# An idle tile at the right end of SBUF grows from 32 to 416 bytes a partition, in a one-core encoder layer

## The chip, the core and the metric

The kernel runs on one core of a Trainium2 chip. The metric is the device time of one execution in microseconds, as the median of several runs. On-chip memory (SBUF) has 128 partitions; an address below is a byte offset within a partition, the same in all of them. TensorE (PE in the profile) multiplies a 128x128 block of weights, loaded by an instruction of its own (PEld), with a stream of up to 512 columns, and writes to PSUM. DVE, ACT and POOL are the vector, scalar and GpSimd engines, and SP issues transfers.

## What is computed

One layer of an encoder on a 1024 x 1024 float32 activation: a feed-forward half step, a mixing step of two groups of attention heads, and a second feed-forward half step, each between two RMS norms.

```python
def swiglu(x, w_gate, w_up, w_down):
    return (jax.nn.silu(x @ w_gate) * (x @ w_up)) @ w_down      # d_ff = 2816

h = swiglu(rmsnorm(x, ffn1_pre_g), ffn1_w_gate, ffn1_w_up, ffn1_w_down)
x = x + 0.5 * rmsnorm(h, ffn1_post_g)
h = rmsnorm(x, mix_pre_g)
q, k, v = split(h @ w_qkv)                     # 16 heads of 64
o_na = neighbourhood_attention(q[:8], k[:8], v[:8], na_rel_bias)
o_dil = dilated_mixture_attention(q[8:], k[8:], v[8:], t5_rel_bias)
mixed = concat(rmsnorm(o_na, na_out_g), rmsnorm(o_dil, dil_out_g)) @ w_out
x = x + rmsnorm(mixed, mix_post_g)
h = swiglu(rmsnorm(x, ffn2_pre_g), ffn2_w_gate, ffn2_w_up, ffn2_w_down)
x = x + 0.5 * rmsnorm(h, ffn2_post_g)
```

## The kernel before

**Products.** Every float32 operand is split into a high part and a remainder (`hi`, `lo`), and one product of 128 x 128 weights and 512 columns becomes three on TensorE: hi x hi, hi x lo, lo x hi (`mm3`, lines 340 to 344; the profile's L342, L343 and L344). In the code's calls of `matmul(out, a, b)`, `a` is the weights (stationary) and `b` the stream (moving).

**Seven instead of eight.** The large matrix products are cut into 2 x 2 blocks and done in a scheme with seven block products of sums and differences, named A11, A12, S1, S2, S3, S4 and A22 after their left operand. The x operand of each is held in SBUF as a `hi` and a `lo` tile of 8192 bytes a partition (class `Operand`): A11 and A12 in the pool `xa`, the other five in `xb`.

**Gate and up products** (`PairGemm`, PSUM tiles `mmp`). One pass over 22 blocks in each FFN, and over 8 blocks for q and k. Weights are the streamed-in matrices, and the 512 columns of x are the stream. In `ahead` (lines 481 to 516) A11 and A12 of the first 10 blocks (8 for q and k) are done early, with weights split into the pool `wr`, or, in the second FFN and for q and k, into the pool `p0` for every third block (line 470 ff.). Then `run` (lines 561 to 625) does the remaining products block by block: an early block has S2, S1, S3, S4 and A22, a late one all seven. In late blocks the order on TensorE is A11, A22 of the block before, S2, A12, S1, S3, S4; each is 4 steps of k times three products, 12 products of 512 columns. Weights for S2, S1 and S3 (`T2`, `T1` in the code) are split into the pool `wt`; those for A11, A12, S4 and A22 into `wr`. While a block's products run, ACT and DVE split the next block's weights (L441, L442) out of the raw tiles of `wg`, and DVE forms their sums and differences (L530 to L532). The first two blocks of the first FFN do A11 in two halves of 256 columns.

**Down and value products** (`Passes`, PSUM tiles `accp`). Here the seven products run as seven passes, and both operands (`pw`) are fetched and split into tiles of the pool `pr` (L722, L723), except in the value passes, where x of `Operand` is the weights and `pw` alone is the stream. In the value passes the first fetch of A11 goes to `p0` (`pw0hi`, `pw0lo`) and the second to a tile of `xb`.

**Attention.** Per head: scores (`sp`, L1121 and L1239), softmax, transposes (`ptp`, L1038), copies to `pt` (L1040) in the pool `ptp`, and products with v (`po`, L1142 and L1255) of 128 columns. v is held in `va` and `vb`, or `vs`, from the pool `vp0`, for every second pair of dilated heads from `op`.

**Order.** The order on TensorE is the program's. The other engines' order is found by the framework, with some places tied by hand. A tile may take the place of earlier ones as soon as those are done with; this wait is found tile by tile, from the addresses (`reuse_waits="tile"`).

**Where tiles lie.** Pools are stacked from both ends of SBUF. From the left: 16,384 bytes that are reserved, 128 bytes of constants, the identity (512 bytes, at 16,512), and the pool `small` (960 bytes), so that the next left pool begins at 17,984, which is 35 x 512 + 64. From the right end, 229,344, first comes the tile `edge` with 32 bytes, so that the next right pool ends at 229,312, which is 447 x 512 + 448. Tiles of products and their raw inputs have sizes that are multiples of 512, hence all left ones lie at 64 modulo 512 and all right ones at 448, with the exceptions in the table.

| tiles | end | address modulo 512 |
|---|---|---|
| x of S1, S2, S3, S4, A22 (`xb`); `wr`, `pr`, `pw`; `sp`, `cp`; operands of the output projection | left | 64 |
| x of A11, A12 (`xa`); `wt` of the two FFNs; `p0`; `wg` and `tj` while the blocks run; `st` (pool `stk`), `vp0`, `og` | right | 448 |
| `wt` and `wg` for q and k after the early blocks | left | 64 |
| `pt` (pool `ptp`), `s` and `sb` (pool `pp`), two of four `pb` | right, behind `at` with 1,152 bytes | 320 |
| `q`, `va`, `vb` of the pool `op`, behind two `ob` of 4,224 bytes | left | 320 |
| identity (the stream of the transposes) | left | 128 |

The lines that the change touches are 1332, where `edge` is made, and 1746 and 1747, where the pools `at`, `pp` and `ptp` are opened, all in `layer`.

Of the kernel before, what the change touches and what calls it, by code (L numbers as in the profile page):

```python
# [10 lines left out]
F32 = mybir.dt.float32  # L11
# [8 lines left out]
P, T = 128, 512  # L20
# [1292 lines left out]
def layer(tc, a, out):  # L1313
    nc = tc.nc
    c = Ctx(tc)
    with ExitStack() as ctx:
        def pool(name, bufs, stack=ctx, **kw):
            return stack.enter_context(tc.tile_pool(name=name, bufs=bufs, reuse_waits="tile", **kw))
# [10 lines left out]

        c.dr = pool("dr", 1, space=bass.MemoryType.DRAM)  # L1330
        c.base = pool("base", 1)
        pool("edge", 1, side="right").tile([P, 8], F32, name="edge")
        c.small = pool("small", 4)
        c.ident = c.base.tile([P, P], F32, name="ident")
        make_identity(nc, c.ident)
# [409 lines left out]
        og = c.og = [ogp.tile([P, 8, 512], F32, name=f"og{g}") for g in range(2)]  # L1745
        for n, b in (("at", 2), ("pp", 4), ("ptp", 3)):
            setattr(c, n, pool(n, b, s4, side="right"))
        for n, b, st in (("pst", 2, s7), ("pss", 3, s5), ("pso", 2, s5), ("psm", 1, s5)):
            setattr(c, n, pool(n, b, st, space=PSUM))
        xo = {}  # L1750
# [198 lines left out]
```

## Time and profile before

| | |
|---|---|
| median of 3 runs | 1877.63 us (1876.08 to 1878.42) |
| the profiled execution | 1875.7 us |
| its span in the profile | 1873.9 us, 25125 instructions |
| mean granted TensorE clock | 0.998 of full speed |
| products of 128x512 as `mmp` | 3 lines x 1464 less 3 x 16 of 256 columns |
| products of 128x512 as `accp` | 3 lines x (600 + 104 + 128 + 24) |

Stages, as the trace has them: up to 445 us the gate and up products of the first FFN (the early A11 and A12 up to 60), then its down passes to some 640, v and q, k to 910, attention to 1130, output projection to 1220, gate and up of the second FFN to 1655, down passes to the end.

How to read it: a group of instructions is a line of the code, an engine, an operation, and output <- inputs by tile names with numbers left out; then count, busy time, mean duration in ns of one, and the idle time before them with what ended it. Products are pipelined, so a duration overlaps the next product's; the distance from start to start is what a product takes. The profile shows tile names, no addresses; those come from the pools, as above.

### The profile page before, as it was taken

Reading aid. Unit: us, or ns where it says so; the run is one execution under the profiler, and the core shown is the slowest. Engines: PE = TensorE matmul, PEld = TensorE weight load, DVE = VectorE, ACT = ScalarE, POOL = GpSimd, SP = SyncE. Lnnn points to the kernel's source line nnn. Section 1 sums busy time; section 2 is a strip of 40 time slices with the busy share of each in tenths; the row PEclk is TensorE's granted clock in tenths of the full one; section 3 lists DMA queues with packets and bytes.
Section 4 is the critical chain, followed back from the end, with each engine's and each line's share of the span. In section 5 each row is a group of like instructions: output and inputs, shape, how many; then the busy total and the mean of one; then the engine's idle time right before and its main releaser. Section 6 shows DMA issues by size and latency. Waiting matters only on the chain.

```text
span 1873.9 us, 25125 instructions
## 1 busy us (share of the span) xinstructions
PE 1837.1 (98%) x8904; PEld 1527.2 (81%) x8904; DVE 1332.9 (71%) x2247; ACT 829.3 (44%) x1485; POOL 321.1 (17%) x504
## 2 busy tenths in 40 slices
PE   8999999999999999999999999999999999999998
PEld 6787888887888887878899997877888888878886
DVE  6878777776466877577777856788886777754558
ACT  6522233334443656133688765563223333344333
POOL 2123111111121122132333100120111111110000
PEclk9999999999999999999999999999999999999999
DMA  7656455546889857769686522584554566486564
GB/s 281 235 167 218 147 211 203 219 180 236 312 294 312 288 206 245 256 209 304 201 276 223 186 96 101 192 303 153 187 179 166 181 213 230 179 325 203 193 227 141
DMA packets 171808, 406.52 MB, mean 217 GB/s; under 512 B 19921, under 2 KB 42353, under 8 KB 169634
## 3 DMA queue, kind: packets, MB, share of 16 engines
q1 hardware_dynamic: 123842, 244.23, 39.3%
q0 software_dynamic: 46832, 158.59, 23.0%
q10 hardware_dynamic: 1008, 2.10, 0.3%
q8 instruction: 70, 1.15, 0.2%
q14 instruction: 56, 0.46, 0.1%
HBM read 278.39 MB, written 131.52 MB: 219 GB/s over the span
## 4 chain that ended last, share of the span: by engine, by line
PE 73%; issue 12%; DVE 8%; DMA 3%; ACT 2%; POOL 1%; SPq 0%; DVEq 0%; POOLq 0%; ACTq 0%
PE mmp L344 16%; PE mmp L343 16%; PE mmp L342 16%; PE accp L343 5%; PE accp L344 5%; PE accp L342 5%; PE po L1142 2%; PE po L1255 2%; PE ptp L1038 2%; DMA x<-x 1%; PE sp L1239 1%; DVE pw L723 1%; PE sp L1121 1%; PE trp L173 1%; DVE x L290 1%
## 5 line engine op out<-in xcount | busy, mean ns | idle before, releaser
L342 PE MATMUL mmp<-x,whi 128*128 128x512 f32 (+1 forms) x1464 | 578.3, 395 | 4.4 <-ACT whi L441 3.0
L344 PE MATMUL mmp<-x,wlo 128*128 128x512 f32 (+1 forms) x1464 | 575.7, 393 | 3.6 <-DVE wlo L442 3.6
L343 PE MATMUL mmp<-x,whi 128*128 128x512 f32 (+1 forms) x1464 | 575.2, 393 | 0.8 <-DVE x L181 0.7
L342 PEld LDWEIGHTS mmp<-x,whi 128*128 128x128 f32 x1464 | 276.4, 189 | 68.4 <-issue 3.4
L344 PEld LDWEIGHTS mmp<-x,wlo 128*128 128x128 f32 x1464 | 276.4, 189 | 68.2 <-DVE wlo L442 5.9
L343 PEld LDWEIGHTS mmp<-x,whi 128*128 128x128 f32 x1464 | 276.5, 189 | 63.0 <-DVE x L181 1.6
L723 DVE TENSOR_TENSOR pw<-praw,pw 128x1024 fp32r<-128x1024 f32 (+1 forms) x181 | 200.5, 1149 | 120.1 <-ACT pw L722 119.8
L722 ACT CAST pw<-praw 128x1024 fp32r<-128x1024 f32 (+1 forms) x181 | 168.5, 981 | 209.3 <-PE accp L344 171.7
L343 PE MATMUL accp<-pw 128*128 128x512 f32 x600 | 233.7, 389 | 3.4 <-DVE pw L723 3.4
L441 ACT CAST whi<-wraw 128x1024 fp32r<-128x1024 f32 x128 | 134.4, 1051 | 230.0 <-PE mmp L343 223.4
L342 PE MATMUL accp<-pw 128*128 128x512 f32 x600 | 234.4, 391 | 0.5 <-DVE hb L779 0.5
L344 PE MATMUL accp<-pw 128*128 128x512 f32 x600 | 233.6, 389 | 0.0
L442 DVE TENSOR_TENSOR wlo<-wraw,whi 128x1024 fp32r<-128x1024 f32 x128 | 157.2, 1230 | 22.3 <-ACT whi L441 22.1
L343 PEld LDWEIGHTS accp<-pw 128*128 128x128 f32 x600 | 112.7, 188 | 27.2 <-DVE pw L723 4.2
L342 PEld LDWEIGHTS accp<-pw 128*128 128x128 f32 x600 | 112.6, 188 | 24.4 <-issue 0.9
L344 PEld LDWEIGHTS accp<-pw 128*128 128x128 f32 x600 | 112.6, 188 | 23.4
L619 DVE TENSOR_TENSOR c<-mmp,u 128x512 f32<-128x512 f32 x52 | 36.0, 692 | 90.0 <-PE mmp L344 90.0
L667 POOL DMA_DIRECT2D g<-sg x44 | 23.9, 543 | 443.7 <-DVE sg L660 263.2
L441 ACT CAST whi<-traw 128x512 fp32r<-128x512 f32 x52 | 32.3, 621 | 151.2 <-DVE traw L531 106.8
L460 ACT COPY s<-mmp 128x512 f32<-128x512 f32 x52 | 30.6, 588 | 133.5 <-PE mmp L344 122.4
L530 DVE TENSOR_TENSOR wraw<-wraw 128x1024 f32<-128x1024 f32 x52 | 63.5, 1222 | 8.7 <-DMA wraw<-in_wu_dram 7.7
L605 DVE TENSOR_TENSOR c<-mmp,v 128x512 f32<-128x512 f32 x52 | 35.8, 689 | 35.9 <-PE mmp L344 34.8
(282 smaller groups left out, 2768.5 us busy)
## 6 DMA issues: line engine op xcount, KB each, us to landing
praw<-g SPq DMA_DIRECT2D x70, 512.0 KB, 5.9
wraw<-in_wg_dram SPq DMA_DIRECT2D x44, 512.0 KB, 4.3
wraw<-in_wu_dram SPq DMA_DIRECT2D x44, 512.0 KB, 6.6
tr<-in_wd_dram SPq DMA_DIRECT2D x44, 512.0 KB, 6.4
g<-sg POOLq DMA_DIRECT2D x88, 256.0 KB, 5.2
ts<-tr POOLq DMA_DIRECT2D x22, 1024.0 KB, 4.7
praw<-ts SPq DMA_DIRECT2D x88, 256.0 KB, 4.0
praw<-in_wd_dram SPq DMA_DIRECT2D x66, 256.0 KB, 5.9
```

Source lines behind the costliest of these rows:

```text
L342: nc.tensor.matmul(out, ahi, bhi, start=start, stop=False, skip_group_check=go_on)
L343: nc.tensor.matmul(out, ahi, blo, start=False, stop=False, skip_group_check=go_on)
L344: nc.tensor.matmul(out, alo, bhi, start=False, stop=stop, skip_group_check=go_on)
L441: nc.scalar.copy(hi, raw)
L442: nc.vector.tensor_sub(lo, raw, hi.bitcast(F32))
L530: nc.vector.tensor_sub(r[:, 0:2], r[:, 1:3], r[:, 0:2])
L619: nc.vector.tensor_add(c21, d, u2)
L722: nc.scalar.copy(hi, raw[:, :m])
L723: nc.vector.tensor_sub(lo, raw[:, :m], hi.bitcast(F32))
L1038: nc.tensor.transpose(ps[:, j, :], src[:, j * P:(j + 1) * P], c.ident)
L1142: nc.tensor.matmul(po[:, un * 2 + j], pt[:, 2 * j + t, :], rhs, start=t == 0, stop=t == 1)
L1255: nc.tensor.matmul(po[0][:, u], pt[0][:, j, :], vs[:, k0 + j, :], start=j == 0, stop=j == n - 1)
```

## The change

```diff
@@ -1329,7 +1329,7 @@
 
         c.dr = pool("dr", 1, space=bass.MemoryType.DRAM)
         c.base = pool("base", 1)
-        pool("edge", 1, side="right").tile([P, 8], F32, name="edge")
+        pool("edge", 1, side="right").tile([P, 104], F32, name="edge")
         c.small = pool("small", 4)
         c.ident = c.base.tile([P, P], F32, name="ident")
         make_identity(nc, c.ident)
@@ -1745,6 +1745,8 @@
         og = c.og = [ogp.tile([P, 8, 512], F32, name=f"og{g}") for g in range(2)]
         for n, b in (("at", 2), ("pp", 4), ("ptp", 3)):
             setattr(c, n, pool(n, b, s4, side="right"))
+            if n == "at":
+                c.at.tile([P, 96], F32, tag="edge", name="edge", bufs=1)
         for n, b, st in (("pst", 2, s7), ("pss", 3, s5), ("pso", 2, s5), ("psm", 1, s5)):
             setattr(c, n, pool(n, b, st, space=PSUM))
         xo = {}
```

The tile `edge` takes 416 bytes instead of 32, so every tile from the right end lies 384 bytes lower, at 64 modulo 512 where it lay at 448. In the attention the pool `at` gets a tile of 384 bytes that nothing reads or writes; `pp` and `ptp`, stacked behind it, lie 768 bytes lower in all, at 64 where they lay at 320. Left tiles stay, those of `op` at 320 among them. The lowest tile of `ptp` then begins at 124,480, where the left tile `hs` of the output projection ends. No instruction is added or removed.

## The prediction

> **What bounds the kernel now.** I read the page's busy times first, then the chain of waits, then the costliest groups, and last the stretches and single products that these point to.
>
> ```profile
> span 1873.9 us, 25125 instructions
> PE 1837.1 (98%) x8904; PEld 1527.2 (81%) x8904; DVE 1332.9 (71%) x2247; ACT 829.3 (44%) x1485; POOL 321.1 (17%) x504
> PE 73%; issue 12%; DVE 8%; DMA 3%; ACT 2%; POOL 1%; SPq 0%; DVEq 0%; POOLq 0%; ACTq 0%
> ```
>
> PE has something in flight for 98% of the span and is 73% of the chain that ended last. Only 1873.9 - 1837.1 = 36.8 us of the span has no product in it. So a time can change in two ways: the products get closer together or farther apart, or a wait appears. The groups say which products these are:
>
> ```profile
> L342 PE MATMUL mmp<-x,whi 128*128 128x512 f32 (+1 forms) x1464 | 578.3, 395 | 4.4 <-ACT whi L441 3.0
> L344 PE MATMUL mmp<-x,wlo 128*128 128x512 f32 (+1 forms) x1464 | 575.7, 393 | 3.6 <-DVE wlo L442 3.6
> L343 PE MATMUL mmp<-x,whi 128*128 128x512 f32 (+1 forms) x1464 | 575.2, 393 | 0.8 <-DVE x L181 0.7
> L342 PEld LDWEIGHTS mmp<-x,whi 128*128 128x128 f32 x1464 | 276.4, 189 | 68.4 <-issue 3.4
> L343 PE MATMUL accp<-pw 128*128 128x512 f32 x600 | 233.7, 389 | 3.4 <-DVE pw L723 3.4
> L342 PE MATMUL accp<-pw 128*128 128x512 f32 x600 | 234.4, 391 | 0.5 <-DVE hb L779 0.5
> L344 PE MATMUL accp<-pw 128*128 128x512 f32 x600 | 233.6, 389 | 0.0
> ```
>
> The same 128x512 product has a mean of 393 to 395 ns as `mmp` and 389 to 391 ns as `accp`, and neither group waits for anyone worth naming (4.4 us at most in 1464). A duration here holds the product's tail under the next one, so the distance between starts is the real price; it is read from stretches and start times:
>
> ```profile
> 250.00:445.00 195.00, 195.00 (x844) 158.20 (x843) 142.62 (x171) 65.99 (x90) 26.51 (x45) 1.00 0.56 204
> 500.00:600.00 100.00, 100.00 (x443) 82.84 (x442) 61.54 (x64) 41.10 (x52) 19.01 (x24) 1.00 0.83 286
> 1700.00:1800.00 100.00, 100.00 (x443) 82.81 (x442) 49.57 (x52) 41.34 (x52) 0.00 (x0) 1.00 0.58 193
> ```
>
> The columns are the stretch, its length, then busy time and count of PE, PEld, DVE, ACT and POOL, the granted clock, and DMA. PE is never idle in the three, and the clock is full. A stretch also counts products cut at its ends, up to two: 195 us over 843 is 231.3 ns a product in the gate products, 100 us over 441 is 226.8 ns in the passes. The same product, at the same clock, is 4.5 ns dearer in one stage than in the other.
>
> **Which products are the dear ones.** In the late blocks of a gate GEMM the runs are known from the code (S1 and S3 with 24 products, then S4, A11, the last block's A22, S2, A12 with 12 each), so the first product of each run can be found in the order of time:
>
> ```profile
> 330.91 0.40 PE L342 MATMUL mmp<-x,whi 128*128 128x512 f32 x1
> ...
> 336.50 0.40 PE L342 MATMUL mmp<-x,whi 128*128 128x512 f32 x1
> ...
> 339.26 0.40 PE L342 MATMUL mmp<-x,whi 128*128 128x512 f32 x1
> ...
> 342.05 0.39 PE L342 MATMUL mmp<-x,whi 128*128 128x512 f32 x1
> ...
> 344.79 0.40 PE L342 MATMUL mmp<-x,whi 128*128 128x512 f32 x1
> ...
> 347.59 0.39 PE L342 MATMUL mmp<-x,whi 128*128 128x512 f32 x1
> ...
> 350.36 0.40 PE L342 MATMUL mmp<-x,whi 128*128 128x512 f32 x1
> ```
>
> Now lay the addresses beside it. Left tiles lie at 64 modulo 512, right ones at 448. S1 and S3 take weights from `wt` (right) and x from `xb` (left): 5.59 us for 24, or 232.9 ns. A11 (weights left, x right) takes 2.79 us for 12, 232.5 ns; S2 (weights right, x left) 2.80, 233.3 ns; A12 2.77, 230.8 ns. I call these 60 **mixed**; together 13.95 us, 232.5 ns each. S4 and A22 have both operands on the left: 2.76 us, 230.0 ns, and 2.74 us, 228.3 ns. They come right behind mixed runs; the passes, where nothing is mixed, have 226.8. So the price goes with the two residues differing, and a run of equal residues needs a dozen products or more to come down.
>
> Is it the residue, or which end of SBUF an operand lies in? In the value passes the first fetched pair has both at 448: weights are x of A11 (right), the stream is `pw0` out of `p0` (right).
>
> ```profile
> 674.62 0.39 PE L342 MATMUL accp<-pw0hi,x 128*128 128x512 f32 x1
> ...
> 679.83 0.39 PE L344 MATMUL accp<-pw0hi,x 128*128 128x512 f32 x1
> ```
>
> From the first to the 24th start are 5.21 us, 226.5 ns a product: 448 with 448 is as quick as 64 with 64. These weights lie near 196,500 to 208,300 and the stream near 129,000 to 137,000. Later in the value passes both are on the left, far apart: x of S2, S1 and S4 as weights between 18,000 and 84,000, the stream out of `pr` between 138,800 and 159,300.
>
> ```profile
> 766.00 0.39 PE L342 MATMUL accp<-pw,x 128*128 128x512 f32 x1
> ...
> 786.40 0.39 PE L342 MATMUL accp<-pw,x 128*128 128x512 f32 x1
> ```
>
> 20.40 us for 90 products, 226.7 ns. So a long distance costs nothing, and wherever a border between two parts of SBUF might lie, from 18,000 to 208,300, one of these two pairs crosses it without a price. The residue is what is left.
>
> **The change part by part.** No instruction is added, removed or moved: two tiles that nobody reads or writes grow or appear. What moves is addresses. Every right tile goes down by 384 bytes, 448 to 64; `pp` and `ptp` go down by 768, 320 to 64. All 512-column products then have equal residues.
>
> Count of mixed products (12 for each run of four k, times three). Each FFN: S2, S1, S3 in 22 blocks, 792, and A11, A12 in the 12 late blocks, 288; twice that is 2160. A11 and A12 of the early blocks: first FFN 10 x 24 less the 24 that run as halves of 256 columns, 216; second FFN 6 x 24 = 144, since four blocks have their weights in `p0`, right as x is; q and k 5 x 24 = 120 (their `wt` is left). Value passes 72 of 336. Sum 2712 of the 6912 products of 512 columns.
>
> Term 1, mixed products: 232.5 - 226.7 = 5.8 ns each. I leave out the 192 of q, k and v, whose stretch is not bound by PE:
>
> ```profile
> 640.00:780.00 140.00, 137.35 (x623) 111.23 (x622) 99.26 (x164) 75.10 (x125) 35.78 (x60) 1.00 0.74 254
> 697.46 6.81 DMA graw<-in_wqk_dram
> 740.76 6.07 DMA qk<-qk
> ```
>
> The two lower rows are pieces of the chain of waits there, start and length: it runs through DMAs, 1.1 us at stake (192 x 5.8). So 2520 x 5.8 = 14.6 us.
>
> Term 2, runs of equal residues behind mixed ones: S4 and A22 lose (230.0 - 226.7) x 12 = 40 ns and (228.3 - 226.7) x 12 = 19 ns a block. Over 44 blocks, 2.6 us come back.
>
> Term 3, the other way: a run that starts after short products is out of step as well. Between the products stand transposes, in groups of four:
>
> ```profile
> L173 PE MATMUL trp<-ident,x 128*128 128x128 f32 x144 | 21.8, 276 | 2.5 <-DVE x L290 1.6 <-DVE x L221 0.5 <-ACT raw L255 0.4
> L173 PE MATMUL trp<-ident,xn 128*128 128x128 f32 x48 | 7.9, 298 | 1.7 <-DVE xn L1586 0.9 <-DVE x L290 0.8
> ```
>
> That is 192 / 4 = 48 groups. If each leaves the next run to settle at S4's 40 ns, 1.9 us stay. Bounds: 0 if it settles at once, 3.8 if it takes twice as long; I take the middle since S4 is the nearest row.
>
> Small products of the attention change residues too, and some pairs that agree now will differ (`pt` goes 320 to 64, while `va` and `vb` out of the pool `op` stay at 320). The two rows are `vb` out of `vp0` (448, differs from `pt`) and out of `op` (320, the same):
>
> ```profile
> L1142 PE MATMUL po<-vb,pt 128*128 128x128 f32 x64 | 8.5, 275 | 0.0
> ...
> L1142 PE MATMUL po<-vb,pt 128*128 128x128 f32 x32 | 4.2, 275 | 0.0
> ```
>
> 275 ns both ways: no price, a zero that needs no cover.
>
> DVE and ACT keep their operands' sizes. Their rows with one residue for all (L723 in the passes, mostly left) and with two (L442, `wraw` right and `whi` left or right):
>
> ```profile
> L723 DVE TENSOR_TENSOR pw<-praw,pw 128x1024 fp32r<-128x1024 f32 x153 | 182.9, 1233 | 116.7 <-ACT pw L722 116.4
> L442 DVE TENSOR_TENSOR wlo<-wraw,whi 128x1024 fp32r<-128x1024 f32 x128 | 157.2, 1230 | 22.3 <-ACT whi L441 22.1
> L722 ACT CAST pw<-praw 128x1024 fp32r<-128x1024 f32 x153 | 153.2, 1047 | 201.4 <-PE accp L344 170.1 <-DMA praw<-in_wd_dram 19.5 <-DMA praw<-g 6.1
> L441 ACT CAST whi<-wraw 128x1024 fp32r<-128x1024 f32 x128 | 134.4, 1051 | 230.0 <-PE mmp L343 223.4 <-issue 4.0 <-DMA sgt<-sgd 2.1
> ```
>
> 0.3% apart: nothing. Waits for a reused place: right tiles now begin where left tiles end (both 64 modulo 512) instead of 384 bytes above, so a right tile laps over as many old left tiles as before or one fewer. No wait can be added between them; I count zero.
>
> Sum: 14.6 + 2.6 - 1.9 = 15.3 us. A second way, from the groups' means: mmp (395 + 393 + 393) / 3 = 393.7 against accp 389.7, 4.0 ns over 4392 products, is 17.6 us, without term 3. The profiled execution took 1875.7 us, 1.8 us of it outside its span; 1875.7 - 15.3 = 1860.4. The median of the three runs is 1.9 us higher, so **1862.3 us**.
>
> [...]
>
> **Rivals.** A (partly): the products close up, but where PE already waits, others take the gain. PE's gaps are in three more stretches:
>
> ```profile
> 25.00:60.00 35.00, 34.10 (x158) 27.29 (x158) 26.73 (x55) 23.99 (x40) 9.36 (x18) 1.00 0.86 315
> 60.00:250.00 190.00, 186.38 (x799) 149.18 (x798) 147.74 (x198) 55.98 (x77) 45.02 (x81) 0.99 0.56 188
> 1200.00:1290.00 90.00, 86.37 (x400) 69.15 (x399) 70.97 (x119) 52.85 (x90) 21.57 (x40) 1.00 0.71 250
> ```
>
> DVE is at 76 to 79% there, which speaks for it; that PE's idle is 4% or less speaks against. Mixed there: 216 + 10 blocks x 36 + 144 = 720, 4.2 us lost, so 1866.5.
>
> B (not the residue): the 5.8 ns hang on something that the shift leaves, as on weights and stream coming from two pools. For it: in every mixed run the two come from different ends. Against: S1 of the value passes takes weights from `xb` and its stream from `pr`, two pools far apart, at 226.7. Nothing would change: 1877.6.
>
> C (slower): with all residues equal, the streams of PE meet those of DVE and ACT, which now lie at 64 too, in the gate stage's splits. Price: if all 6912 products then cost the mixed price, the 4200 cheap ones lose 5.8 ns, 24.4 us, so 1877.6 + 24.4 = 1902.0; it decides from 15.3 us / 6912 = 2.2 ns a product. Against: between 500 and 600 us raw, split and streamed operands all are left tiles, DVE is busy for 61.54 and ACT for 41.10 us, and the product takes 226.8.
>
> **How the numbers follow.** Forecast 0.78, A 0.12, B 0.06, C 0.04. Faster or slower begins at 0.2%, 3.8 us, about what a measurement of this kernel can tell from no change. Forecast and A are faster: 0.90; B is within: 0.06; C is slower: 0.04. The range: at the low end all of 17.6, the 1.1 of q, k and v, and 1.4 for the spread of the three runs (1876.08 to 1878.42), 1857.5; at the high end A with twice the settling (1.9) on top, 1868.4, taken as 1868.5. It leaves out B and C.
>
> **What would show it.** The mean of `mmp` falls to 389 to 390 ns in all three lines; a block of 84 products (350.36 - 330.91 = 19.45 us now) takes 84 x 226.7 = 19.04; the passes and the attention stay as long as they are; PE's idle time stays near 37 us. Wrong: `mmp` still at 393 or more (B), `accp` above 391 (C), or shorter products with PE's idle grown by 4 us (A).

## The result, and the profile after

| | before | after |
|---|---|---|
| median, runs taken together | 1878.03 us (1876.08 to 1879.09) | 1862.49 us (1859.45 to 1862.71) |
| the profiled execution / its span | 1875.7 / 1873.9 us | 1862.6 / 1860.8 us |

The ratio is 0.9915, with a 95% interval of 0.9898 to 0.9932: 15.5 us less, where 15.3 were forecast. The page of the changed kernel, busy times, chain of waits and the groups of the large products:

```profile
span 1860.8 us, 25124 instructions
PE 1820.4 (98%) x8904; PEld 1526.4 (82%) x8904; DVE 1329.6 (71%) x2247; ACT 830.7 (45%) x1485; POOL 321.9 (17%) x504
PE 71%; issue 13%; DVE 8%; DMA 3%; ACT 2%; POOL 1%; SPq 0%; DVEq 0%; POOLq 0%; ACTq 0%
L342 PE MATMUL mmp<-x,whi 128*128 128x512 f32 (+1 forms) x1464 | 573.0, 391 | 5.4 <-ACT whi L441 4.0
L344 PE MATMUL mmp<-x,wlo 128*128 128x512 f32 (+1 forms) x1464 | 571.0, 390 | 4.9 <-DVE wlo L442 4.9
L343 PE MATMUL mmp<-x,whi 128*128 128x512 f32 (+1 forms) x1464 | 570.2, 390 | 0.7 <-DVE x L181 0.6
L343 PE MATMUL accp<-pw 128*128 128x512 f32 x600 | 233.7, 390 | 3.4 <-DVE pw L723 3.4
L342 PE MATMUL accp<-pw 128*128 128x512 f32 x600 | 234.4, 391 | 0.6 <-DVE hb L779 0.6
L344 PE MATMUL accp<-pw 128*128 128x512 f32 x600 | 233.6, 389 | 0.0
```

The instructions are the same (one record is missing in the trace after); of these groups only `mmp` has changed, from 395, 393, 393 ns to 391, 390, 390, and now looks like `accp`, which has not moved. PE's busy time is 16.7 us shorter and the span 13.1: PE's time without a product grew from 36.8 to 40.4 us. The weight loads (PEld) take as long as before, 1527.2 and 1526.4 us; it is the products that follow each other sooner. The order of time has the block that the prediction took apart, first product to first product of the next:

```profile
324.19 0.39 PE L342 MATMUL mmp<-x,whi 128*128 128x512 f32 x1
...
343.23 0.39 PE L342 MATMUL mmp<-x,whi 128*128 128x512 f32 x1
```

19.04 us for 84 products, 226.7 ns each, in place of 19.45. Every one of its seven runs has that price. The stretches of the changed kernel (length; busy time and count of PE, PEld, DVE, ACT, POOL; clock; DMA):

```profile
250.00:440.00 190.00, 190.00 (x840) 157.31 (x839) 140.25 (x170) 65.47 (x89) 26.61 (x45) 1.00 0.57 207
500.00:590.00 90.00, 90.00 (x398) 74.53 (x398) 57.92 (x60) 37.98 (x48) 18.86 (x23) 1.00 0.83 288
```

190 us over 838 and 90 us over 396 are 226.7 and 227.3 ns (a stretch of 90 us reads to half a product): gate products and passes now cost the same. The attention has not moved, here before and after over 220 us, from 910 and from 903 us (PE alone: behind the length stand PE's busy time and count, the clock and DMA):

```profile
910.00:1130.00 220.00, 217.85 (x1759) 1.00 0.60 199
```

```profile
903.00:1123.00 220.00, 217.85 (x1759) 1.00 0.60 199
```

Where this execution gave some of it back shows at two waits. First the stretch behind the start of the q and k blocks' main loop, before and after:

```profile
810.00:825.00 15.00, 13.70 (x61) 11.07 (x60) 12.41 (x16) 6.01 (x7) 3.69 (x5) 1.00 0.42 126
```

```profile
800.00:815.00 15.00, 12.77 (x50) 10.08 (x49) 10.73 (x14) 5.42 (x7) 3.03 (x4) 0.89 0.41 124
```

Eleven products fewer in 15 us, 2.5 us lost. The granted clock differs too, 1.00 before and 0.89 after. The single products after show what happened:

```profile
800.85 0.39 PE L344 MATMUL mmp<-x,wlo 128*128 128x512 f32 x1
803.47 0.47 PE L342 MATMUL mmp<-x,whi 128*128 128x512 f32 x1 [2.23 <-ACT whi L441]
803.77 0.54 PE L343 MATMUL mmp<-x,whi 128*128 128x512 f32 x1
804.11 0.63 PE L344 MATMUL mmp<-x,wlo 128*128 128x512 f32 x1
804.54 0.63 PE L342 MATMUL mmp<-x,whi 128*128 128x512 f32 x1
804.97 0.63 PE L343 MATMUL mmp<-x,whi 128*128 128x512 f32 x1
```

A wait of 2.6 us from start to start, then starts 0.43 us apart, about twice 226.7: the clock record has a window of 3.4 us at half speed from 803.9. Before, the same wait was 1.7 us and no window followed. The chain of waits names what made it longer, a load of the kept A11 product (`s<-s1d`); start and length before and after:

```profile
801.80 7.15 DMA s<-s1d
```

```profile
791.98 8.10 DMA s<-s1d
```

The length of this load is not shown to hang on the change: in the experiments below it is 7.07 us with equal residues (e1) and 8.01 us with residues 32 apart (e5).

The second place is the start of the second FFN's main loop: 2.1 us of waiting before, with no half clock, 2.2 us after, with one from 1274.9. There 8 us hold 20 products instead of 27, 1.6 us lost. Before had one such window inside the kernel, at 74.6 us, behind a wait of 3.2 us. After has none there, though the same wait is 3.5 us long. From 17 us on, where both clock records run, the two profiles have 12 waits of over 2 us from start to start, 2.1 to 3.5 us long. Each of the three windows stands at one of them and begins between 0.1 us before its end and 1.4 us after; the other nine have none.

### The profile page after: what moved, and what is told of

Read it like the earlier page. It is cut to its first block, busy times and chain, and to the rows that moved or that the text cites. A ratio compares the mean times of both kernels' runs of the same rounds, so it can differ in the third digit from the quotient of the medians.

```text
span 1860.8 us, 25124 instructions
## 1 busy us (share of the span) xinstructions
PE 1820.4 (98%) x8904; PEld 1526.4 (82%) x8904; DVE 1329.6 (71%) x2247; ACT 830.7 (45%) x1485; POOL 321.9 (17%) x504
## 4 chain that ended last, share of the span: by engine, by line
PE 71%; issue 13%; DVE 8%; DMA 3%; ACT 2%; POOL 1%; SPq 0%; DVEq 0%; POOLq 0%; ACTq 0%
PE mmp L344 15%; PE mmp L343 15%; PE mmp L342 15%; PE accp L343 5%; PE accp L344 5%; PE accp L342 5%; PE po L1142 2%; PE po L1255 2%; PE ptp L1038 2%; DVE pw L723 1%; PE sp L1239 1%; PE sp L1121 1%; DMA x<-x 1%; PE trp L173 1%; DVE wlo L442 1%
## 5 line engine op out<-in xcount | busy, mean ns | idle before, releaser
L723 DVE TENSOR_TENSOR pw<-praw,pw 128x1024 fp32r<-128x1024 f32 (+1 forms) x181 | 200.3, 1148 | 120.5 <-ACT pw L722 120.1
L442 DVE TENSOR_TENSOR wlo<-wraw,whi 128x1024 fp32r<-128x1024 f32 x128 | 157.1, 1229 | 20.8 <-ACT whi L441 19.4
```

What stands on the lines that cost most here:

```text
L442: nc.vector.tensor_sub(lo, raw, hi.bitcast(F32))
L723: nc.vector.tensor_sub(lo, raw[:, :m], hi.bitcast(F32))
```

## The experiments

**Is the attention part of it?**

```diff
-        pool("edge", 1, side="right").tile([P, 8], F32, name="edge")
+        pool("edge", 1, side="right").tile([P, 104], F32, name="edge")
```

> The kernel before with the tile edge at 416 bytes, without the 384 bytes inside the pool at: pp and ptp then lie at 448 modulo 512, every product of 512 columns has equal residues as in the changed kernel. Theory (the gain is the 512-column products' alone): the time of the changed kernel, 1862.5 us, within 2 us, and ratio 0.9915. Rival (the attention's small products are worth part of it): between 1862.5 and 1878, with the attention stage, index by index, longer than in the changed kernel.

Measured 1860.57 us (1860.35 to 1860.91), ratio 0.9909 (0.9894 to 0.9924), the same as the changed kernel within the intervals. The attention, between the same two products some 220 us apart, takes 219.98 us here and 220.00 in the changed kernel. The pad inside `at` is worth nothing; the rival falls.

**Is it the value 64, or the right tiles' place?**

```diff
         c.small = pool("small", 4)
+        c.small.tile([P, 96], F32, tag="pad", name="pad", bufs=1)
```

> The kernel before with edge left at 32 bytes and 384 idle bytes at the left end instead (in the pool small), so that left tiles go from 64 to 448 and right ones stay at 448. Theory (only the difference of the residues counts): as the changed kernel, 1862.5 us within 2 us, mmp at 390 to 391 ns. Rival (the value 64, or moving the right tiles and their waits for reused places, is what helped): about 1878 us, mmp at 393 to 395 ns.

Measured 1863.34 us, ratio 0.9923 (0.9908 to 0.9937). Its page, from the groups:

```profile
L342 PE MATMUL mmp<-x,whi 128*128 128x512 f32 (+1 forms) x1464 | 573.3, 392 | 4.8 <-ACT whi L441 3.3 <-ACT x L180 1.3
L344 PE MATMUL mmp<-x,wlo 128*128 128x512 f32 (+1 forms) x1464 | 570.8, 390 | 4.9 <-DVE wlo L442 4.9
L343 PE MATMUL mmp<-x,whi 128*128 128x512 f32 (+1 forms) x1464 | 570.4, 390 | 0.8 <-DVE x L181 0.7
```

The time is inside the 2 us expected; one of the three lines has 392 ns where 390 to 391 were expected. All operands at 448 are as quick as all at 64 within the intervals, and it was the left tiles that moved. Neither the value nor the moved right tiles with their waits did it; that the two ends agree did.

**Residues apart inside one end.** The changed kernel, with idle bytes that move single pools (here 128; the next runs differ in the two numbers):

```diff
             c.wr, c.cp, c.sp = pool("wr", 1, w), pool("cp", 2, w), pool("sp", 2, w)
+            c.wr.tile([P, 32], F32, tag="pad", name="pad", bufs=1)
...
                 for h in ("hi", "lo"):
                     c.wt.tile([P, 2, T], F32R, tag="m" + h, name="place")
+                c.wt.tile([P, 32], F32, tag="pad", name="pad", bufs=1)
```

> The changed kernel with 128 idle bytes put into two pools of the gate stages, wr (while run works) and wt: weights of S4, A22 and of the late A11, A12 lie 128 above the stream's residue (1632 products), those of S1 and S3 128 below (1056), those of S2 stay equal. S4 and A22 are pairs within the left end. Theory (residue): 2688 products are mixed again at +5.8 ns, 15.6 us, so 1876 to 1879 us; S4 and A22 now cost 231 to 234 ns a product although both operands are left tiles. Rival (the ends or pools count, not the residue): no change, 1862.5 us, S4 and A22 at 226.7.

Measured 1879.74 us, ratio 1.0008 to before (0.9998 to 1.0017): the whole gain is gone with 256 idle bytes in two pools. The time is 0.7 us above the range expected. The first products of S1, S4 and A11 in one block:

```profile
332.64 0.39 PE L342 MATMUL mmp<-x,whi 128*128 128x512 f32 x1
...
338.22 0.40 PE L342 MATMUL mmp<-x,whi 128*128 128x512 f32 x1
...
341.00 0.40 PE L342 MATMUL mmp<-x,whi 128*128 128x512 f32 x1
```

S4, with both operands on the left, takes 2.78 us for 12 products, 231.7 ns, where it took 226.7 in the changed kernel; S1 and S3 take 5.58 for 24, 232.5. So it is not the ends of SBUF nor the pools: rival B's mechanism falls a second time.

**How does the price go with the distance?**

> As the run with 128 bytes, with 64: the same 2688 products, residues 64 apart. If any difference modulo 512 costs the same: 1876 to 1879 us and 231 to 234 ns. If only steps of 128 bytes or more count: 1862.5 us and 226.7 ns. If the cost grows with the difference: about half of it, 1870 us and 229 to 230 ns.

Measured 1876.30 us, ratio 0.9997 (0.9987 to 1.0006).

```profile
330.73 0.40 PE L342 MATMUL mmp<-x,whi 128*128 128x512 f32 x1
...
336.24 0.39 PE L342 MATMUL mmp<-x,whi 128*128 128x512 f32 x1
...
339.04 0.39 PE L342 MATMUL mmp<-x,whi 128*128 128x512 f32 x1
```

None of the three readings was right as it stood: S4, 64 above, costs 2.80 / 12 = 233.3 ns, but S1 and S3, 64 below, 5.51 / 24 = 229.6. The time is at the low end of the first reading. The sign matters.

> The changed kernel with 32 idle bytes in wr and in wt: weights 32 bytes above the stream's residue in S4, A22 and the late A11, A12, 32 below in S1 and S3. With 64 bytes, above cost 233.4 ns and below 229.3. If the difference in whole words of 64 bytes counts, 32 is as good as none: 226.7 to 227.5 ns, 1862 us. If any difference counts: above 231 to 234, below 228 to 230 ns, 1872 to 1877 us.

Measured 1879.70 us, ratio 1.0012 (1.0002 to 1.0023). First products of S1, S4 and A11:

```profile
333.58 0.40 PE L342 MATMUL mmp<-x,whi 128*128 128x512 f32 x1
...
339.19 0.39 PE L342 MATMUL mmp<-x,whi 128*128 128x512 f32 x1
...
341.98 0.40 PE L342 MATMUL mmp<-x,whi 128*128 128x512 f32 x1
```

32 bytes are enough: S1 and S3, 32 below, take 5.61 / 24 = 233.8 ns here, S4, 32 above, 2.79 / 12 = 232.5. Of the three numbers expected for "any difference" only the price above holds: minus 32 is not cheap, and so the time is above the 1872 to 1877 us.

> As before with 192 bytes, so +192 and -192 (320 modulo 512). If any difference above 64 costs alike: 232 to 233.5 ns in both, 1877 to 1880 us. If the cost comes back with every 128 bytes, plus 192 is as plus 64 (233.4) and minus 192 as minus 64 (229.3): 1875 to 1877 us.

Measured 1873.06 us, ratio 0.9976 (0.9965 to 0.9986). First products of S1, S4, A22 and S2:

```profile
329.85 0.40 PE L342 MATMUL mmp<-x,whi 128*128 128x512 f32 x1
...
335.45 0.40 PE L342 MATMUL mmp<-x,whi 128*128 128x512 f32 x1
...
340.96 0.39 PE L342 MATMUL mmp<-x,whi 128*128 128x512 f32 x1
343.71 0.40 PE L342 MATMUL mmp<-x,whi 128*128 128x512 f32 x1
```

Neither expected time was met; it is lower than both. A22, 192 above, costs 2.75 / 12 = 229.2 ns, as 64 below did (229.6 in e4); S1 and S3, 192 below, 5.60 / 24 = 233.3, as 64 above did (233.3). Plus 192 and minus 64 are 256 apart, so a period of 256 explains both; a period of 128 would need plus 64 and minus 64 to be alike, which they are not (233.3 and 229.6).

> As before with 256 bytes in wr and 160 in wt: +256 in S4, A22, late A11 and A12, -160 in S1 and S3. If what counts is the residue modulo 256, +256 is free: 226.7 ns in those four, and only S1 and S3 (1056 products) cost, so 1868 us. If it is modulo 512: 232 to 233.5 ns in all six, 1877 to 1880 us.

Measured 1872.62 us, ratio 0.9969 (0.9958 to 0.9980). First products of S1, S4, A11 and S2:

```profile
331.35 0.39 PE L342 MATMUL mmp<-x,whi 128*128 128x512 f32 x1
...
336.96 0.39 PE L342 MATMUL mmp<-x,whi 128*128 128x512 f32 x1
...
339.70 0.39 PE L342 MATMUL mmp<-x,whi 128*128 128x512 f32 x1
...
345.14 0.39 PE L342 MATMUL mmp<-x,whi 128*128 128x512 f32 x1
```

A11 and A22, both 256 apart, take 5.44 us for 24, 226.7 ns: free. S4, also 256 apart, has 2.74 / 12 = 228.3, since it stands behind S1 and S3, which at 160 below cost 5.61 / 24 = 233.8. The time is some 4.6 us above the 1868 expected: 1056 products at +7.1 ns are 7.5 us, settling of S4 adds 1.6 x 12 x 44 = 0.8, so 1870.8; the remaining 1.8 us are within the spread of the runs (1868.86 to 1874.79).

The prices of the runs together, as mean distance of starts over all products of a kind whose neighbours have the same difference, weights less stream (S4 of e7 and S2 of e3 to e6, which settle behind other residues, left out):

```
difference, modulo 256      ns a product   seen in
0 (also 256)                226.7-226.8    changed kernel, block loops; e7: A11, A12, A22
32                          232.8-233.3    e5: S4, A22, A11, A12
64 (also 320)               233.3-233.6    e4: S4, A22, A11, A12; e6: S1, S3
96 (as 352)                 234.0          e7: S1, S3
128 (also 384)              231.8-233.4    before; e3: all six
192 (also 448)              228.7-230.0    e6: S4, A22, A11, A12; e4: S1, S3
224 (as 480)                233.2-233.5    e5: S1, S3
```

**The same in the passes.** The changed kernel, with 128 bytes between the two halves of a `pw` tile:

```diff
-            w = c.pr.tile([P, 1 + self.own, 2, 2, T], F32R, tag="w", name="pw")
-            w = [[w[:, side, h] for h in range(2)] for side in range(1 + self.own)]
+            n = 4 * T
+            w = c.pr.tile([P, n + self.own * (n + 32)], F32R, tag="w", name="pw")
+            w = [w[:, side * (n + 32):][:, :n].rearrange("p (h i x) -> p h i x", h=2, i=2) for side in range(1 + self.own)]
+            w = [[x[:, h] for h in range(2)] for x in w]
```

> The changed kernel with 128 idle bytes between the weights' and the stream's half of each pw tile in the down passes: 1752 products there get residues 128 apart, 384 modulo 512. Theory (the price belongs to the pair of residues, not to the gate stages): the passes cost 232 to 233 ns a product instead of 226.7, 1752 x 5.8 = 10.2 us, so 1871 to 1874 us. Rival (the gate stages with their sums and evictions are what is sensitive): 226.7 ns and 1862 us.

Measured 1870.51 us, ratio 0.9960 (0.9947 to 0.9974): 8.0 us slower than the changed kernel, a little under the range.

```profile
1700.00:1800.00 100.00, 100.00 (x433) 80.96 (x432) 53.87 (x59) 42.42 (x58) 0.00 (x0) 1.00 0.59 195
```

100 us over 431 is 232.0 ns: the passes, untouched so far, take the same price as soon as their operands differ. The price by the stretch is 5.2 ns, so 1752 x 5.2 = 9.1 us.

**Is a period of 256 enough for the whole kernel?**

```diff
-        pool("edge", 1, side="right").tile([P, 8], F32, name="edge")
+        pool("edge", 1, side="right").tile([P, 40], F32, name="edge")
```

> The kernel before with edge at 160 bytes and nothing else: right tiles at 320 modulo 512, left at 64, 2712 products with residues 256 apart. Theory (only the difference modulo 256 counts): as the changed kernel, 1860 to 1863 us, all products at 226.7 to 227 ns. Rival (modulo 512, and the 226.7 seen at 256 apart holds only within the left end or beside equal ones): 1870 us or more.

Measured 1863.48 us (1862.66 to 1865.37), ratio 0.9926 (0.9913 to 0.9940). The stretch of the gate products, PE alone:

```profile
250.00:440.00 190.00, 190.00 (x840) 1.00 0.58 209
```

The same 840 products in 190 us as in the changed kernel. The median is 1 us over it and 0.5 over the range expected, and the intervals overlap. Over the whole trace the 2637 products 256 apart that follow each other without a wait have a mean of 227.0 ns, as the equal ones have.

**The half clock.** Seven products that nobody reads are put into each of the two waits:

```diff
+    def warm(self, n, a, b):
+        c = self.c
+        ps = c.pst.tile([P, 4, P], F32, tag="tr", name="warm").rearrange("p a b -> p (a b)")
+        for _ in range(n):
+            c.nc.tensor.matmul(ps, self.op.x[a][0][:, 0, :P], self.op.x[b][0][:, 0, :], start=True, stop=True)
...
+            if b == 0 and self.fill == "run":
+                self.warm(7, A11, A12)
...
+            if b == 0 and self.fill == "s4":
+                self.warm(7, S1, S3)
```

> The changed kernel with seven products of 512 columns (1.6 us) that nobody reads, put on TensorE where it waits: before the first product of the second FFN's main loop, and before S4 of the first block of q and k. In the changed kernel's profile both waits (2.2 and 2.6 us) are followed by a window of 3.4 us at half the granted clock, 1.6 to 1.8 us lost in each. Theory (the idle time causes the half clock, which takes back part of the gain): the windows near 804 and 1275 us go, 1859 to 1860 us. Rival (the windows come from something else): they stay, and the time is 1862 to 1863 us or, where the seven products outlast the wait, up to 1864.

Measured 1861.29 us (1860.02 to 1864.08), ratio 0.9916 (0.9899 to 0.9932). Stretches around three waits, in the changed kernel and in this one:

```profile
785.00:815.00 30.00, 27.77 (x116) 22.51 (x115) 17.57 (x23) 7.95 (x10) 9.99 (x16) 0.94 0.55 176
1130.00:1145.00 15.00, 11.86 (x71) 9.57 (x70) 11.59 (x40) 5.83 (x21) 0.00 (x0) 1.00 0.00 0
1255.00:1285.00 30.00, 26.52 (x112) 20.92 (x111) 24.40 (x34) 14.76 (x24) 3.25 (x6) 0.94 0.47 168
```

```profile
785.00:815.00 30.00, 29.81 (x133) 24.38 (x132) 19.50 (x25) 8.53 (x10) 9.96 (x16) 1.00 0.56 176
1135.00:1150.00 15.00, 11.86 (x58) 9.26 (x57) 9.93 (x32) 6.08 (x21) 0.05 (x1) 0.89 0.01 1
1255.00:1285.00 30.00, 28.07 (x126) 22.40 (x125) 24.20 (x34) 15.39 (x25) 3.58 (x7) 1.00 0.50 171
```

Where the waits were filled the clock stays at 1.00, as the theory says. But one profile can't show that the filling did it: e1 fills nothing, has the second wait as long as the changed kernel (2.16 us from start to start, at 1271) and the first under 1.7, and the clock stays at 1.00 in both its stretches too:

```profile
785.00:815.00 30.00, 28.78 (x127) 23.55 (x127) 20.08 (x26) 8.02 (x10) 9.96 (x16) 1.00 0.54 170
1255.00:1285.00 30.00, 26.49 (x119) 21.03 (x119) 25.89 (x36) 14.77 (x24) 3.24 (x6) 1.00 0.46 161
```

And the clock fell at a third wait, at the end of the attention (0.89 over 15 us), where the changed kernel's profile has 1.00 over its wait of 2.6 us. So the clock falls at some waits in one execution and at others in the next. What they cost can be estimated: a window of 3.4 us at half speed loses up to 1.7 us and lowers the mean granted clock by 1.7 / 1875 = 0.0009. The runs of the kernel before go that way: those with a mean of 0.999 took 1873.9 to 1874.9 us, those with 0.995 took 1879.1 to 1882.6. That filling two waits pays is not shown: its five runs all have a mean of 0.997, the changed kernel's 0.996 to 0.998, and the median is not told apart from the changed kernel's. The kernels with residues equal modulo 256 (the changed one, e1, e2, e10 and this) lie between 1860.6 and 1863.5 us, with intervals that overlap: none is shown to beat the change.

## Why the prediction was right

**What bounds it, and which products are dear.** Right. The mean of `mmp` fell to 391, 390 and 390 ns, one of the three just above the 389 to 390 forecast. The distance between products fell where the residues had differed and in the equal runs right behind, and hardly elsewhere (0.03 us over all down passes); e3 and e9 bring the price back in other places by addresses alone. The stream of the second value-pass pair reaches to some 163,400, not 159,300 as the prediction has it; its argument on borders stands.

**Term 1, 5.8 ns for a mixed product.** Right in size. Both traces were laid beside each other product by product, waits and half clock left out (distances under 0.3 us). The mixed products (2640 pairs) lay 15.9 us above 226.7 ns each before, 6.0 ns a product, and 0.5 after. Leaving out q, k and v hardly mattered: 0.95 us of the gain are theirs.

**Terms 2 and 3, the settling.** Term 2 is right in size: the products that are equal in both kernels (4076 pairs) lay 4.1 us above 226.7 before and 1.2 after, 2.85 us of gain where 2.6 were counted. Term 3 was too gloomy: the runs that start right behind transposes (45 of them) are some 25 ns dear over their first dozen products, 1.1 us in all, where 40 ns and 1.9 us were counted. Settling itself is shown by S4 in e7, 228.3 ns behind a mixed run, while A11 and A22 at the same distance have 226.7.

**What costs nothing.** Attention: unmoved, as the stretches show, and e1 for the pad in `at`. DVE and ACT: L723 has a mean of 1233 ns before and 1232 after, L442 1230 and 1229; busy are DVE 1332.9 and 1329.6 us, ACT 829.3 and 830.7. No new wait for a reused place turned up, and e2, which moves the other end, has the same time within the intervals.

**The sum.** Products gave 15.35 + 2.85 = 18.2 us in the profiled execution, more than the 15.3 of the sum; 5.1 were given back there, 3.6 as idle time (36.8 to 40.4) and some 1.6 at half clock, since it has two such windows inside where before had one. The two waits shown cost 4.1 of it; the window at 74.6 us, which only before had, sets 1.6 against them, and the rest is smaller waits. The prediction named rival A for gains lost at waits, but for another reason (DVE at the start of each FFN), and priced no clock. So in the profile 13.1 us are left. The medians differ by 15.5. That 1862.3 and 1862.49 lie so close is in part luck: the products gave some 3 us more than was counted, and waits and half clock, counted at nothing, took about as much back.

**Rivals.** A: its sign, PE's idle time grown by 4 us, nearly came (3.6, where none was forecast), but at other waits, and the medians differ by the whole 15.5. B: refuted by the result, then by e3 within one end. Products whose residues differ take 2 to 7 ns more than others, while a weight load of `mmp` has a mean of 189 ns before and after; whether the price comes from the loads or from the streams, no run here shows. C: refuted: all operands now share one residue with what DVE and ACT read and write, and the products cost 226.7.

## What to carry to other kernels

All of this is from one kernel on one core. Where TensorE is the bound and products of 512 float32 columns follow each other, compare the distance of starts between stages; if it differs at full clock, work out the residue modulo 256 of the weights' and of the stream's addresses. A few idle bytes at the end of a pool can be worth most of a per cent, as here (0.85%), and a pool with a size that isn't a multiple of 256 in front of operands can cost as much: 128 idle bytes in each of two pools took the changed kernel's 1862.49 us to 1879.74 in e3. Price it per product from a run where the residues agree, and allow for settling (five to eight products here), but look also at the waits, since a gain that is spread over thousands of products can come back at one wait in whole microseconds (2.5 us here, at the start of the q and k blocks' main loop).

## What was not expected of the hardware

- In these kernels the period is 256 bytes, not 512: operands 256 apart cost 226.7 ns like equal ones, in e7 and over the whole kernel in e10 (1863.48 us with an edge of 160 bytes).
- It is neither a step nor symmetric: 32 bytes cost as much as 128 (233 and 232 ns), while weights 64 below the stream cost 229.3 ns and 64 above 233.4. Why was not tried, and which memory structure lies behind it stays open; only distances in steps of 32 were measured, and 160 is not among them.
- A run of equal residues behind a mixed one starts dear (232 ns for the first two products in S4 and A22 of the kernel before) and comes down to 226.7 ns, after five products in S4 of e7 and after eight in S4 and A22 of the kernel before. What settles there stays open.
- At three of the 12 waits of over 2 us in the profiles before and after, the granted clock was 0.5 for 3.4 us. In the changed kernel's profile this happened at a wait of 2.2 us that passed without it before, at 2.1, and in e1, at the same 2.2. What decides between the two stays open.
